# Sixteen output gates of a hybrid decoder layer, moved from the heads' stage into a Strassen product by token

## The chip, the cores and the metric

One core of a Trainium2 chip runs the whole layer as one program. The metric is the device time of one launch in microseconds; the kernel before takes 2931.25 us (median of three runs, 2930.26 to 2932.18). Names of engines: PE is TensorE, DVE is VectorE, ACT is ScalarE, POOL is GpSimd, SP is SyncE, whose queue issues every DMA of this kernel.

## The reference

One layer on 512 tokens of width 2048, float32. After an adaptive RMS norm, h is multiplied by one wide matrix w_in whose columns feed all that follows:

- a sliding-window attention branch with 32 query heads, gated by silu and projected to y_a;
- a gated DeltaNet branch with 16 key heads and 32 value heads of 128 columns. A causal convolution and silu give q, k and v, a recurrence over chunks gives o for each value head, and then

```python
o = rms_norm(o, dn_norm_w) * silu(dz.reshape(B, T, DN_V_HEADS, DN_HEAD_V))
y_b = o.reshape(B, T, DN_VAL) @ w_o_dn
```

- a merge y = sigmoid(mg_a) * y_a + sigmoid(mg_b) * y_b, and x + gate * (y @ w_out).

The change concerns dz = h @ w_in[:, 12800:16896], 128 columns for each value head: the output gates.

## The kernel before, in words

**Products.** h lies transposed in SBUF (channels on partitions, tokens along the row) as two parts, hh (rounded to a shorter format) and hl (the rest). A weight is split the same way: ACT rounds a half tile of 128 x 1024 into whi (split, L52) and DVE subtracts into wlo (L53). Each product of such operands takes three matmuls (mm3, L237): high by high, high by low, low by high. A **channel tile** (channel_tile, L244) computes 128 output channels for all 512 tokens: 16 steps over the input channels, 48 matmuls into one PSUM bank. `plan` (L158) lists the weight tiles in the order of use; raw tiles of 1 MB are loaded two ahead (load_job, L195), their halves are split with three buffers (split_half, L204).

**Order of work.** Everything that hangs beside the large products is written as a generator, and `pump` (L81), called after every second step of a channel tile (eight times per tile), advances it: `live` generators count their waits in calls of pump, `slow` ones (the triangular solve) have a budget per call, and `side` ones (beside, L78) a rate per call. The program's scheduler then orders each engine's instructions by this order and by when it expects their inputs.

**The heads' stage** (deltanet, L590; heads, L788). For each of 16 key heads g there are five channel tiles: the queries q, two value heads v, and two gates z. `queries` (L818) runs the convolution, transposes, masks (POOL, L714 and L715), the product pqk (L869), the assembly of the inverse, and then `scan` (L898), the recurrence over four chunks, in which PE, DVE and ACT take turns. `zgate` (L797) turns a z tile into silu times the norm's weight, still with channels on partitions. At the end of scan the two heads' results in osb (tokens on partitions) are scaled by the norm (L968), turned on PE (transpose4, L271, tiles pto), multiplied by the gate on DVE (L975) and stored to o_d (L979). The solve of the second half of the heads runs as a slow generator in groups 0 to 7 and is drained at g = 8 (L643).

**Behind it** branch_b (L982) loads o_d head by head (L996), splits it, runs merge tiles ma5 to ma8 and multiplies by w_o_dn; attention (L1063) runs ma9 to ma15 at its end (L1101), while the last heads finish; finish (L1271) ends with the output product (output, L1326). That product is already a Strassen step: 512 x 2048 x 2048 as seven products of quadrants (256 tokens, 1024 input channels, 1024 output columns, in two column halves of 512). Its **items** are twelve matmuls of 128 x 512 each, four items to a product (m1 to m7), with tokens as output partitions. Weight quadrants lie in three slots a, b, c and are summed in place on DVE (L1347).

Of the kernel before, what the change touches and what calls it, by code (L numbers as in the profile page):

```python
# [16 lines left out]
P = 128  # L17
# [16 lines left out]
STW = 320 + NST * P  # L34


class Layer:
# [120 lines left out]
    def plan(self):  # L158
        a, jobs = self.a, []
        wi = lambda name, t: jobs.append((name, a["w_ch"][t]))  # L160
        jobs += [(f"st{u}", a["w_st"][u]) for u in range(KT // 2)]
        for j in range(NFIRST):
            wi(f"mb{j}", 96 + j)
        for kind, j in self.mixed():
            wi(f"{kind}{j}", (16 if kind == "k" else 96) + j)
        ma = lambda r: [wi(f"ma{j}", 146 + j) for j in r]
        ma(range(0, 3))
        for g in range(KH):
            wi(f"q{g}", g)
            for e in (2 * g, 2 * g + 1):  # L170
                wi(f"v{e}", 32 + e)
            for e in (2 * g, 2 * g + 1):
                wi(f"z{e}", 64 + e)
        ma(range(3, 5))
        for half in range(2):
            ma(range(5 + 2 * half, 7 + 2 * half))
# [8 lines left out]
        ma(range(9, 16))  # L185
        jobs += [(f"os{j}", a["w_os"][j]) for j in range(KT)]
        self.jobs = jobs

    def prime(self):
        self.job_load = self.half_split = self.half_used = 0  # L190
        self.raws, self.halves, self.due = {}, {}, []
        for _ in range(2):
            self.load_job()

    def load_job(self):  # L195
        j = self.job_load
        if j < len(self.jobs):
# [6 lines left out]
    def split_half(self):  # L204
        n = self.half_split
        j = n // 2
        if j < len(self.jobs):
# [7 lines left out]
            if n % 2:  # L215
                del self.raws[j]
                self.due.append(self.load_job)

# [25 lines left out]
    def channel_tile(self, name, xh=None, xl=None):  # L244

        xh, xl = (self.hh, self.hl) if xh is None else (xh, xl)
        ps = self.pmm.tile([P, T], F32, tag="mm", name="mm")
# [29 lines left out]
    def build(self):  # L277
        tc, nc, a = self.tc, self.nc, self.a
        with ExitStack() as es:
# [26 lines left out]
            if self.stop == "deltanet":  # L306
                return
            self.gate_d = self.dram.tile([D], F32, name="gate_d")
# [9 lines left out]
    def consts(self):  # L318
# [20 lines left out]
        nc.vector.tensor_scalar(out=self.dnwh, in0=self.dnw, scalar1=0.5, scalar2=None, op0=ALU.mult)  # L339
        yield  # L340
# [249 lines left out]
    def deltanet(self):  # L590
# [8 lines left out]
        self.o_d = dram.tile([VH, P, T], F32, name="o_d")  # L599
        with ExitStack() as ps:  # L600
# [34 lines left out]
            with ExitStack() as sb:  # L635
# [12 lines left out]
                self.drain_live()  # L648
        self.dump("o", self.o_d)
# [138 lines left out]
    def heads(self, wk, g):  # L788
# [5 lines left out]
        for e in range(2):  # L794
# [12 lines left out]
    def values(self, wk, g, e, ps, st):  # L807
# [6 lines left out]
        vt = wk.tile([P, NTB, P], F32, tag="vt", name="vt", bufs=3)  # L814
# [3 lines left out]
    def queries(self, wk, g, ps, st):  # L818
# [22 lines left out]
        for e in range(2):  # L841
            h = 2 * g + e
            qe = wk.tile([P, NTB, P], F32, tag="qe", name="qe", bufs=2)
# [54 lines left out]
    def scan(self, wk, g, k, kT, TT, qd, M, epsq, st):  # L898
# [3 lines left out]
        osb = wk.tile([P, 2, NTB, P], F32, tag="osb", name="osb", bufs=1)  # L902
# [53 lines left out]
        while len(z) < 2:  # L956
# [9 lines left out]
        for e in range(2):  # L966
# [3 lines left out]
            )  # L970
        yield 2
# [8 lines left out]


    def branch_b(self):  # L982
        tc, nc, a = self.tc, self.nc, self.a
        with ExitStack() as es:
# [8 lines left out]
            for half in range(2):  # L993
# [4 lines left out]
                for j in range(2):  # L998
                    self.merge_gate("ma", 5 + 2 * half + j, self.ma_d)
# [63 lines left out]
    def attention(self):  # L1063
        tc, nc, a = self.tc, self.nc, self.a
        with ExitStack() as es:
# [35 lines left out]
            for j in range(9, KT):  # L1101
# [388 lines left out]
def layout(i):  # L1490
# [18 lines left out]
    o["w_ch"] = f(np.concatenate([ch(w_in[:, 4608:16896]), ch(w_in[:, 19008:]), ch(w_in[:, :2304]), ch(w_in[:, 2560:4608]), ch(w_in[:, 16960:19008])]))  # L1509
    o["w_os"] = f(ch(i["w_o_swa"][0]))  # L1510
# [57 lines left out]
```

## Time and profile before

| what | value |
|---|---|
| median of 3 runs | 2931.25 us |
| span of the profiled execution (the page gives it no other time) | 2929.7 us |
| PE, DVE, ACT, POOL busy | 98%, 61%, 37%, 8% of the span |
| heads' stage, one steady period | 67.31 us |
| output stage, first and second column half | 90.5 and 78.7 us |
| loads and stores | 451.11 MB, mean 154 GB/s |

How to read it: a row of the profile names a line of the kernel, an engine, an operation, the tile written and the tiles read; then come the count, the busy time, the mean of one in nanoseconds, the idle time of the engine just before, and what ended that idle time. A stretch row gives its length and then the busy time and the instruction count of each engine, the granted clock of PE (1.00 is full), the DMA engines' busy share and their rate. Consecutive matmuls overlap, so the busy time of one (0.39 us) is more than its share of the time.

### The profile page before, as it was taken

The numbers are of one execution on the slowest core, as the hardware profiler recorded it, in microseconds if no ns is written. First come the engines' busy times: TensorE is split into PE (matmuls) and PEld (weight loads), VectorE is DVE, ScalarE is ACT, GpSimd is POOL, SyncE is SP. The second block draws the span as 40 slices with busy tenths as digits, with TensorE's granted clock in tenths as the row PEclk, the third lists the DMA queues.
The fourth block names the chain that finished last, engine by engine and source line by source line (L and its number), as shares of the span: only waits on it lengthen the run. The fifth ranks groups of instructions, "written<-read, shape, count | busy, mean of one in ns | idle before, by whom it ended". The sixth has DMA issues, their size and how long they took to land.

```text
span 2929.7 us, 38073 instructions
## 1 busy us (share of the span) xinstructions
PE 2870.6 (98%) x14556; PEld 2351.2 (80%) x14556; DVE 1787.2 (61%) x2915; ACT 1085.1 (37%) x2113; POOL 243.0 (8%) x204
## 2 busy tenths in 40 slices
PE   8899999999999999999999999999999999999988
PEld 6677888888888888888888788888787877888867
DVE  6775998777776545544444553434655655553697
ACT  4355333333334333333333322212343443432343
POOL 0022211100000110000000000000100000000022
PEclk9999999999999999999999999999999999999999
DMA  9747555633334533333332675554322223375562
GB/s 387 281 147 219 163 169 159 203 109 111 125 113 134 160 116 124 115 122 109 123 109 100 235 263 182 186 172 141 105 89 94 85 89 103 119 262 172 173 194 97
DMA packets 175046, 451.11 MB, mean 154 GB/s; under 512 B 72433, under 2 KB 74993, under 8 KB 138897
## 3 DMA queue, kind: packets, MB, share of 16 engines
q1 hardware_dynamic: 174866, 448.70, 46.1%
q8 instruction: 114, 1.87, 0.3%
q14 instruction: 66, 0.54, 0.1%
HBM read 386.95 MB, written 59.45 MB: 152 GB/s over the span
## 4 chain that ended last, share of the span: by engine, by line
PE 84%; DVE 3%; DMA 2%; issue 1%; ACT 1%; POOL 1%; SPq 0%; POOLq 0%; DVEq 0%; ACTq 0%
PE mm L240 24%; PE mm L242 24%; PE mm L241 24%; DVE wlo L53 1%; PE S L1208 1%; PE pv L918 1%; PE po L937 1%; PE O L1259 1%; PE pP L274 1%; PE po L936 1%; PE pd L933 1%; PE pp L908 1%; PE m L241 1%; PE m L242 1%; PE m L240 1%
## 5 line engine op out<-in xcount | busy, mean ns | idle before, releaser
L240 PE MATMUL mm<-hh,whi 128*128 128x512 f32 x2784 | 1130.7, 406 | 2.3 <-ACT whi L52 1.6
L242 PE MATMUL mm<-hh,wlo 128*128 128x512 f32 x2784 | 1089.6, 391 | 1.3 <-DVE wlo L53 1.3
L241 PE MATMUL mm<-hl,whi 128*128 128x512 f32 x2784 | 1087.3, 391 | 0.0
L53 DVE TENSOR_TENSOR wlo<-raw,whi 128x1024 fp32r<-128x1024 f32 (+1 forms) x452 | 554.4, 1229 | 491.5 <-ACT whi L52 481.7
L52 ACT CAST whi<-raw 128x1024 fp32r<-128x1024 f32 (+1 forms) x452 | 470.7, 1044 | 972.9 <-PE mm L241 927.3
L242 PEld LDWEIGHTS mm<-hh,wlo 128*128 128x128 f32 x2784 | 522.6, 188 | 115.1 <-DVE wlo L53 2.2
L240 PEld LDWEIGHTS mm<-hh,whi 128*128 128x128 f32 x2784 | 523.7, 188 | 112.3 <-issue 8.4
L241 PEld LDWEIGHTS mm<-hl,whi 128*128 128x128 f32 x2784 | 524.2, 188 | 98.7 <-issue 0.4
L240 PE MATMUL mm<-oh,whi 128*128 128x512 f32 x512 | 200.6, 393 | 2.6 <-ACT oh L52 1.7
L242 PE MATMUL mm<-oh,wlo 128*128 128x512 f32 x512 | 199.4, 390 | 0.5 <-DVE wlo L53 0.5
L241 PE MATMUL mm<-ol,whi 128*128 128x512 f32 x512 | 199.5, 390 | 0.1
L865 POOL TENSOR_TENSOR qe<-qe,yq 128x512 f32<-128x512 f32 x32 | 51.4, 1624 | 902.7 <-DMA qe<-eg_rows 836.9
L714 POOL TENSOR_TENSOR E<-E,neg_g 128x512 f32<-128x512 f32 x64 | 78.4, 1224 | 476.2 <-DMA E<-g_rows 342.8
L240 PEld LDWEIGHTS mm<-oh,whi 128*128 128x128 f32 x512 | 96.0, 188 | 24.8 <-ACT oh L52 3.0
L241 PEld LDWEIGHTS mm<-ol,whi 128*128 128x128 f32 x512 | 96.1, 188 | 22.2 <-DVE ol L53 1.3
L764 DVE TENSOR_TENSOR A<-A,atmp 128x62 f32<-128x62 f32 (+30 forms) x124 | 112.9, 911 | 1.5
L242 PEld LDWEIGHTS mm<-oh,wlo 128*128 128x128 f32 x512 | 96.1, 188 | 20.9 <-DVE wlo L53 1.3
L757 DVE TENSOR_TENSOR atmp<-A 128x62 f32<-128x62 f32 (+30 forms) x124 | 109.3, 882 | 1.5
L911 DVE SCALAR_TENSOR_TENSOR r<-pp,neg_eg,vt 128x128 f32<-128x128 f32 x96 | 29.2, 346 | 78.8 <-PE pp L908 77.6
L1232 ACT ACTIVATE sm<-sm,mx,rs 128x256 f32<-128x256 f32 (+1 forms) x128 | 71.7, 561 | 3.3 <-DVE mx L1227 3.3
L580 DVE SCALAR_TENSOR_TENSOR yv<-mm,convh,yv 128x511 f32<-128x511 f32 (+2 forms) x96 | 71.5, 745 | 1.6
L241 PE MATMUL m<-wlo,hh 128*128 128x512 f32 x128 | 51.8, 404 | 10.1 <-DVE wlo L53 10.1
(331 smaller groups left out, 3145.6 us busy)
## 6 DMA issues: line engine op xcount, KB each, us to landing
raw<-in_w_ch SPq DMA_DIRECT2D x158, 1024.0 KB
wa<-in_w_ada_ss SPq DMA_DIRECT2D x32, 1024.0 KB
raw<-in_w_od SPq DMA_DIRECT2D x32, 1024.0 KB
E<-g_rows SPq DMA_DIRECT2D x64, 256.0 KB
gw<-in_w_ada_gate SPq DMA_DIRECT2D x16, 1024.0 KB
raw<-in_w_os SPq DMA_DIRECT2D x16, 1024.0 KB
qe<-eg_rows SPq DMA_DIRECT2D x32, 256.0 KB
o_d<-zh SPq DMA_DIRECT2D x32, 256.0 KB
```

Source lines behind the costliest of these rows:

```text
L52: self.nc.scalar.copy(out=hi, in_=src)
L53: self.nc.vector.tensor_tensor(out=lo, in0=src, in1=hi.bitcast(F32), op=ALU.subtract)
L240: nc.tensor.matmul(ps, lhsT=wh, rhs=xh, start=first, stop=False)
L241: nc.tensor.matmul(ps, lhsT=wh, rhs=xl, start=False, stop=False)
L242: self.last_mm = nc.tensor.matmul(ps, lhsT=wl, rhs=xh, start=False, stop=last).ins
L274: self.nc.tensor.transpose(dst[:, c * P : (c + 1) * P], src_cols(c), self.ident)
L580: nc.vector.scalar_tensor_tensor(out=y[:, s:], in0=ps[:, : T - s], scalar=w[:, j : j + 1], in1=y[:, s:], op0=ALU.mult, op1=ALU.add)
L714: nc.gpsimd.tensor_tensor(out=E, in0=E, in1=ng, op=ALU.add)
L757: eng.tensor_tensor(out=t, in0=A[:, m : m + 1, m + 1 :].to_broadcast([P, m, n]), in1=A[:, :m, m : m + 1].to_broadcast([P, m, n]), op=ALU.mult,
L764: eng.tensor_tensor(out=A[:, :m, m + 1 :], in0=A[:, :m, m + 1 :], in1=t, op=ALU.add)
L865: nc.gpsimd.tensor_tensor(out=qf, in0=qf, in1=q, op=ALU.mult)
L1232: nc.scalar.activation(t, t, AF.Exp, scale=r[:, h : h + 1], bias=mx[:, h : h + 1], accum_out=den[:, h : h + 1])
```

## The change

The gates of value heads 12 to 27 (key heads 6 to 13, `ZG`) leave the heads' stage. Their 2048 columns become one product of 512 x 2048 x 2048 in a new stage, zstage, between deltanet and branch_b.

- In groups of ZG heads runs three channel tiles, not five. The scan no longer turns and gates: it stores the scaled osb by token to ot_d, two DMAs per group. Buffers: vt 3 to 4, qe 2 to 4, osb 1 to 2.
- token_sums, a side generator from group 8 on at 0.14 steps per call of pump, makes the four combinations of quadrants of h (s1 to s4) on POOL, DVE and ACT, in four chunks, and stores them as high and low parts (32 stores of 256 KB); the quadrant of h that s1 will replace is saved (two stores of 1 MB).
- zstage loads the weight slots and the sums, runs ma5 (moved here from branch_b) and then 56 items. The sums of weights are issued four items ahead: a+b on DVE, b+c, a+c and b+a on POOL. A finished quadrant is gated by token: tanh on ACT, a multiply-add on DVE, a product with the loaded o on POOL; two items later four transposes on PE, a scaled copy on ACT and the store to o_d. s1 takes the place of a quadrant of hh and hl, which is loaded back in the second half.
- The list of weight loads pauses at zstage and resumes at its end (rejoin). Merge tiles: ma5 to zstage, ma6 to ma9 in branch_b, ma10 to ma15 in attention.

```diff
+Z0 = 12
+ZG = range(Z0 // 2, Z0 // 2 + 8)
...
-            for e in (2 * g, 2 * g + 1):
+            for e in (2 * g, 2 * g + 1) if g not in ZG else ():
                 wi(f"z{e}", 64 + e)
-        ma(range(3, 5))
+        ma(range(3, 6))
+        self.apart = len(jobs)
+        jobs += [(f"za{i}", a["w_z"][0, i]) for i in range(2)]
...
                     if g == 8:
                         self.drain_slow(s1)
+                        self.beside(self.token_sums(sol1), 0.14, "sums")
...
+        if g in ZG:
+            yield 1
+            for e in range(2):
+                k, i = divmod(2 * g + e - Z0, 4)
+                nc.sync.dma_start(
+                    out=self.ot_d[k].rearrange("c p n -> p c n")[:, :, i * P : (i + 1) * P], in_=osb[:, e]
+                )
+            return
...
+            order = [
+                ("m1", "a11", "a", []), ("m7", "s3", "b", ["ab", "bc"]), ("m5", "s1", "a", []), ("m2", "a12", "b", []),
+                ("m6", "s2", "a", ["ac"]), ("m4", "a22", "b", ["ba"]), ("m3", "s4", "c", []),
+            ]
...
+            def weight_sums(i):
+                if i < len(items):
+                    _, m, p = items[i]
+                    for x, y in order[m][3]:
+                        eng = nc.vector if (x, y) == ("a", "b") else nc.gpsimd
+                        eng.tensor_tensor(out=piece(x, p), in0=piece(x, p), in1=piece(y, p), op=ALU.add)
...
+            def turned(k, t, src, scale):
+                pt = pf.tile([P, T], F32, tag="tp", name="ptz", bufs=2)
+                self.transpose4(pt, lambda h: src[:, h * P : (h + 1) * P])
+                oz = wk.tile([P, T], F32, tag="w", name="oz")
+                nc.scalar.activation(oz, pt, AF.Copy, scale=scale)
...
+            def gated(i, n, c, t, src, neg):
+                k = 2 * c + n
+                o = wk.tile([P, T], F32, tag="o", name="ot")
+                nc.sync.dma_start(out=o, in_=self.ot_d[k, t])
+                th = wk.tile([P, T], F32, tag="w", name="zth")
+                nc.scalar.activation(th, src, AF.Tanh, scale=-0.5 if neg else 0.5)
+                nc.vector.scalar_tensor_tensor(out=src, in0=th, scalar=1.0, in1=src, op0=ALU.add, op1=ALU.mult)
+                nc.gpsimd.tensor_tensor(out=src, in0=src, in1=o, op=ALU.mult)
+                late.append((i + 2, k, t, src, self.dnwn if neg else self.dnwh))
...
+                    elif name == "m6":
+                        u1, u5 = keep["m1", t], keep["m5", t]
+                        u = wk.tile([P, T], F32, tag="m", name="u2", bufs=3)
+                        TT(out=u, in0=b, in1=u1, op=ALU.add)
+                        TT(out=u1, in0=ps["m7", t], in1=u, op=ALU.add)
+                        x = wk.tile([P, T], F32, tag="m", name="c22", bufs=3)
+                        TT(out=x, in0=u1, in1=u5, op=ALU.add)
+                        TT(out=u5, in0=u, in1=u5, op=ALU.add)
+                        gated(i, n, 1, 2 + t, x, False)
...
+            load("b", 1, 0, 0)
+            load("c", 1, 1, 0)
+            for n in ("s3", "s2", "s4"):
+                sums(n)
+            pm = self.channel_tile("ma5", ps=pf.tile([P, T], F32, tag="tp", name="ma", bufs=2))
+            th = wk.tile([P, T], F32, tag="w", name="mth")
+            nc.scalar.activation(th, pm, AF.Tanh, scale=0.5)
+            nc.sync.dma_start(out=self.ma_d[5], in_=th)
+            sums("s1")
+            todo = []
+            for i in range(2):
+                slots["a", i] = self.raws.pop(self.apart + i)
...
+                    if kk == 0:
+                        prep(i + 2)
+                        weight_sums(i + 4)
+                        for f in todo:
+                            evict(i, *f)
+                        todo = []
+                        while late and late[0][0] <= i:
+                            turned(*late.pop(0)[1:])
+                if p == 3:
+                    todo.append((n, name))
```

More of the change, by code (lines that the diff above doesn't have):

```diff
@@ L339, in consts @@
         nc.vector.tensor_scalar(out=self.dnwh, in0=self.dnw, scalar1=0.5, scalar2=None, op0=ALU.mult)
+        self.dnwn = const.tile([P, 1], F32, name="dnwn")
+        nc.vector.tensor_scalar(out=self.dnwn, in0=self.dnw, scalar1=-0.5, scalar2=None, op0=ALU.mult)
         yield
@@ L648, in deltanet @@
                 self.drain_live()
+                self.drain("sums")
         self.dump("o", self.o_d)
@@ L901, in scan @@
         v = [st["v0"], st["v1"]]
[L902 removed]
+        osb = wk.tile([P, 2, NTB, P], F32, tag="osb", name="osb", bufs=2)
         osq = wk.tile([P, 2, NTB], F32, tag="osq", name="osq")
@@ L955, in scan @@
         z = st["z"]
-        while len(z) < 2:
+        while g not in ZG and len(z) < 2:
             yield 1
```

179 lines of the change are left out of this document (168 added, 11 removed).

## The prediction

> **What bounds the kernel now.** I read the page's busy shares and its chain first, then stretches of the span by engine, and last the waits and the order of instructions in the stages that the change touches.
>
> ```profile
> span 2929.7 us, 38073 instructions
> ...
> PE 2870.6 (98%) x14556; PEld 2351.2 (80%) x14556; DVE 1787.2 (61%) x2915; ACT 1085.1 (37%) x2113; POOL 243.0 (8%) x204
> ...
> PE 84%; DVE 3%; DMA 2%; issue 1%; ACT 1%; POOL 1%; SPq 0%; POOLq 0%; DVEq 0%; ACTq 0%
> ```
>
> TensorE (PE) is busy for 98% of the span and is 84% of the chain that ended last. The stretches (length, then busy time of each engine with its instructions) show it by stage:
>
> ```profile
> core 0: us, PE busy (x) PEld busy (x) DVE busy (x) ACT busy (x) POOL busy (x), PEclk, DMA share, GB/s
> ...
> 1369.08:1436.39 67.31, 67.31 (x359) 56.03 (x358) 33.52 (x63) 25.12 (x57) 6.45 (x6) 1.00 0.37 119
> 1834.00:2047.00 213.00, 213.00 (x937) 174.95 (x936) 85.73 (x101) 48.56 (x52) 1.00 (x2) 1.00 0.50 167
> 2568.00:2580.00 12.00, 11.25 (x50) 8.98 (x49) 11.22 (x17) 11.13 (x18) 0.00 (x0) 1.00 1.00 355
> 2752.00:2842.50 90.50, 80.37 (x335) 64.03 (x335) 85.85 (x131) 42.10 (x63) 7.73 (x5) 0.94 0.62 201
> 2842.50:2921.20 78.70, 77.12 (x339) 63.16 (x338) 68.56 (x66) 29.36 (x30) 26.23 (x9) 1.00 0.33 106
> ```
>
> The first row is one period of the heads' stage (one key head, two value heads): PE never stops. The second, nearly all large products, gives their price: 213.00 us / 937 = **0.2273 us** each. The last two are the two column halves of the output product, which is already a Strassen step. It is the only place with idle PE time to speak of, and the nearest row for what is added.
>
> **What goes and what comes on PE.** Sixteen gate tiles of 16 x 3 products leave the heads: 768 x 0.2273 = 174.6 us. The new stage has 2 halves x 7 products x 48 = 672, 152.7 us. Gain **21.8 us**. The 64 transposes of these heads move along and cost the same (eight took 1.26 us), and so does the merge tile ma5.
>
> ```profile
> 1626.86 1.26 PE pto L274 x8
> ```
>
> So everything hangs on whether PE stays fed.
>
> **The heads' stage.** A period in groups 6 to 13 falls from 67.31 by 2 x 10.9 and the transposes' 1.3 to about 44.2 us. The scan is emitted by calls of pump, now 24 a group and not 40; from a query tile's end to the last scan step I count some 51, so two groups' scans overlap more. The steps' distance in calls stays, so each has as much PE time over it as before, and the larger buffer counts (vt, qe, osb) fit the overlap. A busier VectorE (DVE) is the risk: 33.52 us less the gates' work (per group four subtractions of weights at 1.24 and four operations of a gate at 0.68, as in these two groups of instructions) is 25.9 in 44.2, 59%, and token_sums adds about 22 us of DVE and 31 of GpSimd (POOL) over groups 8 to 14 (32 operations at 0.68, 24 at the 1.29 below).
>
> ```profile
> L53 DVE TENSOR_TENSOR wlo<-raw,whi 128x1024 fp32r<-128x1024 f32 x436 | 538.1, 1237 | 484.9 <-ACT whi L52 475.2 <-PE pqk L869 5.7 <-PE pgate L1483 3.7
> ...
> L804 DVE SCALAR_TENSOR_TENSOR zh<-zth,zh 128x512 f32<-128x512 f32 x32 | 21.9, 684 | 0.0
> ```
>
> The nearest rows are the early groups, in which the triangular solve keeps DVE fuller still (one product per group starts at these times):
>
> ```profile
> 627.04 0.89 PE pqk L869 x8
> 694.35 0.89 PE pqk L869 x8
> 762.70 0.89 PE pqk L869 x8
> 830.00 0.89 PE pqk L869 x8
> ...
> 1369.08 0.89 PE pqk L869 x8
> ```
>
> Periods of 67.31, 68.35 and 67.30 against the quiet 67.31: at most 1 us lost per group. I take 0.4 for eight groups, **3 us** (0 to 8). The solve itself still ends in time: its last store is issued in group 6, before the forced drain at group 8.
>
> ```profile
> 972.23 1.18 SPq L784 DMA_DIRECT2D ts_d<-A  x2
> ```
>
> SyncE's (SP's) queue gets two stores of osb per group and 34 of sums; what stands behind them are loads a period ahead, and I cost them at nothing. If that cover fails, E and qe are late, and with them the ceiling of 8.
>
> **The new stage: DVE and POOL.** In the old output stage DVE makes all sums of weights; here POOL makes three of four, and multiplies by the heads' result. How these two get on shows in single instructions:
>
> ```profile
> 2850.39 10.36 POOL L1400 TENSOR_TENSOR m<-m,x 128x512 f32<-128x512 f32 x1 [4.52 <-DMA x<-in_x]
> ...
> 2850.44 1.22 DVE L1347 TENSOR_TENSOR raw<-raw,rawb 128x1024 f32<-128x1024 f32 x1
> 2851.58 1.22 DVE L53 TENSOR_TENSOR wlo<-rawb,whi 128x1024 fp32r<-128x1024 f32 x1
> 2852.72 1.22 DVE L1347 TENSOR_TENSOR rawb<-rawb,rawc 128x1024 f32<-128x1024 f32 x1
> ...
> 2859.65 2.18 DVE L53 TENSOR_TENSOR wlo<-rawb,whi 128x1024 fp32r<-128x1024 f32 x1
> ...
> 960.86 3.69 POOL L865 TENSOR_TENSOR qe<-qe,yq 128x512 f32<-128x512 f32 x2 [67.00 <-DMA qe<-eg_rows]
> 961.07 4.55 DVE L777 TENSOR_TENSOR A<-A,bet 128x1024 f32<-128x1024 f32 x2
> ...
> 2904.28 1.29 POOL L1400 TENSOR_TENSOR c<-c,x 128x512 f32<-128x512 f32 x1 [8.54 <-DVE c L1397]
> ...
> 2902.86 0.69 DVE L1425 TENSOR_TENSOR m<-u,m 128x512 f32<-128x512 f32 x1
> 2903.46 0.69 DVE L1397 SCALAR_TENSOR_TENSOR c<-c,gt 128x512 f32<-128x512 f32 x1
> ```
>
> A POOL product of 512 columns takes 1.29 us alone, 10.36 while DVE adds without a gap; a DVE subtraction of 1.22 takes 2.18 when POOL gets in; two of each at 960.86 take turns. They exclude each other. The Trainium skill (SBUF — State Buffer, Who interferes with whom) says so too: a VectorE instruction with two SBUF inputs and a GpSimd instruction that reads SBUF block one another for a whole instruction. By that rule the sums given to POOL are no free second pair of hands, which speaks against this change; the rows agree.
>
> So I add up, per half, what the two need together. Starts in a row give DVE 1.14 us per 1024 columns and 0.60 per 512. POOL's 1024 columns are not in the trace: between 1.29 and twice that, 2.58; I take 2.4, near the upper end, as DVE's own 0.60 and 1.14 nearly double. POOL: 12 x 2.4 + 8 x 1.29 = 39.1. DVE with two SBUF inputs: 28 subtractions and 4 sums x 1.14 + 12 x 0.60 = 43.7. Together **82.8 us**; PE needs 336 x 0.2273 + 32 x 0.16 = 81.5. By the Trainium skill (GPSIMD Engine Reference, 3. Performance versus the Vector engine: 4497 ns for 2048 columns) a sum would be an estimated 2.25, and the total 81.0 instead.
>
> How full can such a pair run? The old second half did (28 + 16) x 1.14 + 12 x 0.60 + 8 x 1.29 = 67.7 in 77.9 us, 87%, and PE waited 1.4:
>
> ```profile
> PE m L241 <- DVE wlo L53: 10.1, 5, 5.9
> ...
> PE m L241 <- DVE wlo L53: 1.4, 1, 1.4
> ```
>
> (The first row is the first half, where DVE makes the operands as well.) At 87% the new half takes 95 us, 13.5 over PE; at 100% 82.8, 1.3 over. The bursts sit around m7 and around m4 and m6, with the weights two items ahead as slack; I take **9 us a half, 18 in all** (3 to 27). ScalarE's queue holds casts behind the tanh of each gate, and PE's transposes stand behind the whole chain DVE, tanh (0.59), DVE, POOL; both are in the 9, since only the chain's lateness against two and a half items (6.8 us) counts. An item, twelve products, is the 2.72 us between two casts:
>
> ```profile
> 2886.50 1.05 ACT L52 CAST whi<-raw 128x1024 fp32r<-128x1024 f32 x1 [1.66 <-PE m L242]
> 2889.22 1.06 ACT L52 CAST whi<-raw 128x1024 fp32r<-128x1024 f32 x1 [1.67 <-PE m L242]
> ...
> L263 ACT ACTIVATE mth<-mm x32: 573/590/632, 156.3 to 2577.4; 128x512 f32<-128x512 f32 x32
> ```
>
> **Its start and end.** The new tiles lie in memory that the last group releases:
>
> ```profile
> L975 DVE TENSOR_TENSOR zh<-pto,zh x32: 677/681/691, 619.7 to 1629.1; 128x512 f32<-128x512 f32 x32
> ```
>
> That is some 4 us after ma5's start. Then b, c, s3, s2, s4 and s1 queue, 12.6 MB: at 355 GB/s (share 1.00 in the row above) 35 us, so s1 is there 39 to 41 us after ma5's start. PE wants it after ma5 and eight items, 10.9 + 21.8 = 32.7, plus a few us of waits: **5 us** (0 to 8). At the end the last gate's chain (two sums 0.60, two tanh, two products, POOL 1.29, transposes, copy) is about 6 us; if the next stage's first bank waits for it, PE stands: **4 us** (0 to 6.5). In attention one merge tile fewer (48 calls, not 56) covers the last group; its last products ended at 2566.2 and the last merge's tanh began at 2577.4 (row above), so of 11 us of cover about none is left: **0.5** (0 to 2).
>
> ```profile
> 2564.31 1.90 PE O L1259 x32
> ```
>
> **Sum.** -21.8 + 3 + 18 + 5 + 4 + 0.5 = **+8.7 us**. On the profiled span, 2929.7, this is 2938.4. The page gives that execution no time beside its span; the median of the runs, 2931.25, is 1.55 above it, so **2940**.
>
> **Rivals.**
> *The cover holds (faster).* Each half waits as little as the old second half, 1.4, because the sums are asked for four items ahead and POOL runs early; s1 is in time and the end is covered: -21.8 + 2.8 + 1 + 1 = -17, **2914**. For it: DVE has half of its time free in the heads, and twelve sums fewer per half here. Against: 82.8 us of mutual exclusion in 81.5.
> *POOL starves and PE stands at the transposes (slower).* Place: m6, where four additions per tile, tanh, gating and POOL's product must be done before PE's turn. Without interference the second tile's source is ready 2.3 (cast and subtraction) + 10 x 0.60 + 1.29 = 9.6 us after the product ends, and PE is there at 6.8 + 0.6 = 7.4; with two sums of 2.4 in between it is 14.4, a wait of 7. With 3 at m3 and 7 at m7 (four sums by each engine and four subtractions, 18.8 us against 10.9 of PE) a half loses 17; two halves and 6 + 6 + 4 for start, end and heads give -21.8 + 50 = +28, **2959**. It decides from where POOL's product starts over 4 us after its inputs.
> *The saving is not collected.* If the scans, not PE, pace the thinner groups, each returns 2.7 us of its 23: -21.8 is gone in the heads alone, and with the stage's waits **2962**.
>
> **Chances.** Forecast (2930 to 2950) 0.47; cover holds 0.25; starved 0.22; not collected 0.06. A difference under 0.2% (5.9 us) can't be told from none. Between 2925.4 and 2937.1 I put 0.13 of the forecast and 0.03 of the first rival: same 0.16, faster 0.22, slower 0.34 + 0.22 + 0.06 = 0.62. Range 2918 to 2962: it leaves out the better half of the first rival (0.13) and the tail of the last two (0.07).
>
> **What would show it.** Periods of 44 to 45 us between the pqk products of groups 7 to 13, not 47, show the gain collected. POOL sums of 2.4 us, several of 4 or more, and DVE subtractions of 2.3 to 3.6 show exclusion. Waits of PE for wlo and for the transposes' sources of 14 to 22 us in all in the new stage, and its length of 185 us without ma5, show the bill. I am wrong if POOL's sums run beside DVE's subtractions at full speed, if the order written by the scheduler keeps all gates off PE's path, or if the loads at the start land in under 33 us.

## The result, and the profile after

The changed kernel takes **2984.5 us** (median of 4 runs, 2979.5 to 2986.9); the kernel before took 2930.8 beside it (4 runs). The ratio is 1.0181, with a 95% interval of 1.0167 to 1.0196. The prediction, 2940 with a range of 2918 to 2962, is outside: right in its sign, 44 us too low.

The page of the changed kernel, in the lines that were shown of before:

```profile
span 2980.9 us, 38256 instructions
...
PE 2870.3 (96%) x14460; PEld 2344.2 (79%) x14460; DVE 1928.4 (65%) x2992; ACT 1124.6 (38%) x2161; POOL 393.9 (13%) x268
...
PE 75%; DVE 6%; DMA 5%; POOL 2%; issue 2%; ACT 1%; SPq 0%; POOLq 0%; DVEq 0%; ACTq 0%
```

PE issues 96 matmuls fewer, as it should, and its busy time is nearly the same; it is less of the chain (75%, not 84%). To see where the time went, I cut both spans at the same work: the product pqk of group 5 (the last with all its gates), the last transposes of the heads (pto), the last of the new stage (ptz). The start of before's first mark; the last heads' transposes of before stand in the prediction, at 1626.86:

```profile
897.77 1.05 PE L869 MATMUL pqk<-yq,kT 128*128 128x128 f32 x8
```

And the changed kernel's three marks (start, length, engine, line; in brackets PE's idle time before and what ended it):

```profile
895.04 1.05 PE L889 MATMUL pqk<-yq,kT 128*128 128x128 f32 x8
...
1484.50 1.26 PE L286 MATMUL pto<-ident,osb 128*128 128x128 f32 x8 [1.30 <-DVE osb L988]
...
1687.82 2.34 PE L286 MATMUL ptz<-ident,m 128*128 128x128 f32 x8 [4.71 <-POOL m L1145]
```

- **Heads.** From pqk to pto before took 1626.86 - 897.77 = 729.1 us, after 589.5: 139.6 less. Gone from PE were 174.6 us of products and the 64 transposes, 10.1, together 184.7. So **45 us were lost in the heads**, where the prediction had 3.
- **New stage.** From the end of pto (1485.76) to the end of ptz (1690.16) are 204.4 us. Its work is ma5 (10.9), 152.7 of products and 10.1 of transposes, 173.7. **31 us were lost**; the prediction had 18 + 5 + 4 = 27. PE is idle for 24 of them; the other 7 go with the granted clock, 0.98 and 0.92 in the two parts below.
- **The rest.** Behind it lie 2980.9 - 1690.2 = 1290.7 us; before, without ma5, 2929.7 - 1628.1 - 10.9 = 1290.7. Nothing was lost there (the prediction had 0.5). The groups ahead of the first mark were 2.7 us shorter.

The waits of PE over the whole run (total, number, longest) name the places:

```profile
PE pd L953 <- DVE vs L945: 28.0, 12, 3.7
...
PE m L253 <- DVE wlo L55: 13.4, 8, 5.3
PE ptz L286 <- POOL c L1145: 10.7, 7, 3.4
PE ptz L286 <- POOL m L1145: 8.6, 3, 4.7
```

The first is a wait that the kernel before doesn't have: a step of the scan, in which PE wants vs. The second was there, mostly in the output stage; only 2.9 us of it lie in the new stage. The last two are the new transposes, which wait for the gate's product on POOL.

Stretches of the changed kernel: groups 6 and 7, two periods of later groups, and the new stage in two parts:

```profile
963.46:1020.34 56.88, 49.88 (x249) 40.47 (x248) 44.09 (x59) 22.78 (x52) 29.55 (x20) 0.91 0.54 173
1020.34:1073.57 53.23, 44.96 (x246) 37.02 (x246) 42.16 (x71) 22.17 (x55) 19.18 (x14) 0.97 0.56 190
...
1073.57:1120.39 46.82, 44.69 (x254) 37.23 (x253) 26.50 (x56) 18.58 (x48) 7.84 (x6) 1.00 0.41 126
1120.39:1168.77 48.38, 46.26 (x254) 38.51 (x253) 26.47 (x56) 18.67 (x48) 7.73 (x6) 0.96 0.38 121
...
1496.50:1596.00 99.50, 89.21 (x391) 71.59 (x389) 81.85 (x56) 43.53 (x50) 52.69 (x21) 0.98 0.60 217
1596.00:1691.00 95.00, 81.25 (x347) 64.75 (x347) 70.20 (x52) 40.34 (x48) 47.04 (x20) 0.92 0.40 123
```

So the heads have two losses of different kinds. In groups 6 and 7 a period is 57 and 53 us, with DVE busy for 44 and 42 of them. In the six periods from 1073.57 to 1358.97 it is 47.6 on the mean (285.4 / 6) where 44.2 was forecast, though DVE has nearly half of its time free. Against the 44.4 us that such a period takes without a wait (run 13), the first two lose 21 us and the six 19; the remaining 4 lie in the period behind them, 71.7 us where before's were 67.3. In the last two rows PE is idle for 10.3 and 13.75 us, and its granted clock is under 1.00.

**Three theories, with rivals.** A: the token sums come as one burst in groups 6 to 8. C: in the later groups some queue holds up the scan, not the scan's work. D and E: in the new stage PE waits for the gate's chain, and that is late because DVE and POOL exclude each other. The rival of A and C is B: without gates the scans themselves are too long for the period.

### The profile page after: what moved, and what is told of

It reads as the page before. It is cut to its first block, busy times and chain, and to the rows that moved or that the text cites. A ratio compares the mean times of both kernels' runs of the same rounds, so it can differ in the third digit from the quotient of the medians.

```text
span 2980.9 us, 38256 instructions
## 1 busy us (share of the span) xinstructions
PE 2870.3 (96%) x14460; PEld 2344.2 (79%) x14460; DVE 1928.4 (65%) x2992; ACT 1124.6 (38%) x2161; POOL 393.9 (13%) x268
## 4 chain that ended last, share of the span: by engine, by line
PE 75%; DVE 6%; DMA 5%; POOL 2%; issue 2%; ACT 1%; SPq 0%; POOLq 0%; DVEq 0%; ACTq 0%
PE mm L252 21%; PE mm L254 21%; PE mm L253 20%; DVE wlo L55 2%; DMA E<-g_rows 2%; PE m L254 1%; PE m L253 1%; PE m L252 1%; PE S L1454 1%; PE po L957 1%; PE O L1505 1%; PE pP L286 1%; PE pd L953 1%; PE pv L938 1%; POOL E L734 1%
## 5 line engine op out<-in xcount | busy, mean ns | idle before, releaser
L252 PE MATMUL mm<-hh,whi 128*128 128x512 f32 x2512 | 1024.1, 408 | 2.3 <-ACT whi L54 1.6
L254 PE MATMUL mm<-hh,wlo 128*128 128x512 f32 x2512 | 985.8, 392 | 1.1 <-DVE wlo L55 1.1
L253 PE MATMUL mm<-hl,whi 128*128 128x512 f32 x2512 | 984.5, 392 | 0.0
L55 DVE TENSOR_TENSOR wlo<-raw,whi 128x1024 fp32r<-128x1024 f32 (+1 forms) x444 | 584.3, 1317 | 439.4 <-ACT whi L54 434.7
L252 PEld LDWEIGHTS mm<-hh,whi 128*128 128x128 f32 x2512 | 475.2, 189 | 103.5 <-issue 8.4
L254 PEld LDWEIGHTS mm<-hh,wlo 128*128 128x128 f32 x2512 | 473.6, 189 | 104.8 <-DVE wlo L55 1.9
L253 PEld LDWEIGHTS mm<-hl,whi 128*128 128x128 f32 x2512 | 475.5, 189 | 89.4 <-issue 0.4
L253 PE MATMUL m<-wlo,hh 128*128 128x512 f32 x256 | 102.6, 401 | 9.0 <-DVE wlo L55 9.0
L254 PE MATMUL m<-whi,hl 128*128 128x512 f32 x256 | 101.8, 398 | 0.9 <-DMA hl<-s_d 0.9
L252 PE MATMUL m<-whi,hh 128*128 128x512 f32 x256 | 101.7, 398 | 0.0
```

The lines of the kernel that those rows point to most:

```text
L55: self.nc.vector.tensor_tensor(out=lo, in0=src, in1=hi.bitcast(F32), op=ALU.subtract)
L252: nc.tensor.matmul(ps, lhsT=wh, rhs=xh, start=first, stop=False)
L253: nc.tensor.matmul(ps, lhsT=wh, rhs=xl, start=False, stop=False)
L254: self.last_mm = nc.tensor.matmul(ps, lhsT=wl, rhs=xh, start=False, stop=last).ins
```

## The experiments

Each run was timed beside the kernel before on the same chip; ratios are to that, and differences from the changed kernel are differences of the ratios (1.0181 less the run's) times 2931 us. Where no edit touches a stage, that stage kept its length within 5 us.

### The burst in groups 6 to 8 (runs 1 and 2)

All operations of the token sums write the tile tsum. Two of their six groups on POOL in the changed kernel (count; shortest, median and longest in ns; first and last start):

```profile
L1033 POOL TENSOR_TENSOR tsum<-hh x4: 1299/1737/1740, 976.1 to 1026.7; 128x512 f32<-128x512 f32 x4
...
L1050 POOL TENSOR_TENSOR tsum<-tsum,hh x4: 1288/1480/1727, 993.6 to 1053.9; 128x512 f32<-128x512 f32 x4
```

All four chunks were done by 1056 us, in group 7, although the generator is advanced at 0.14 steps per call from group 8's emission on. Nothing ties a step to the product beside it; the scheduler puts it where it expects its inputs, and those were there as soon as the solve had stored its half (at 970).

**Run 1** leaves the sums' arithmetic out and keeps their stores, with other data in them (the product is then another one):

```diff
-            for i, v in enumerate((H, L)):
-                PT(out=x[i], in0=v[:, k, lo], in1=v[:, k, hi], op=ALU.add)
-                PT(out=x[2 + i], in0=v[:, k, hi], in1=v[:, u, hi], op=ALU.subtract)
...
+            for n in ("s3", "s1", "s2", "s4"):
+                for j, v in enumerate((H, L)):
+                    nc.sync.dma_start(out=self.ts_sum[n][j, :, k, :], in_=v[:, k, hi])
```

> The token sums' arithmetic is left out of the heads (their 34 stores stay and carry other data, so the product comes out otherwise). Theory A (their 32 VectorE, 24 GpSimd and 16 ScalarE operations come as one burst behind the solve, 963 to 1063 us of the changed kernel, and PE waits for vs there): the periods of groups 5 to 8 fall from some 54 us to the 47 of the later groups, the waits of PE for vs lose the 16 us of that stretch, and the time falls by 14 to 22 us. Rival B (the groups without gates are paced by their scans, whatever lies beside them): the waits move on, and the time falls by 0 to 5 us.

Measured: 2964.5 us, ratio 1.0116 (1.0094 to 1.0138), 19 us less than the changed kernel. The periods from group 6 on are 43.2, 46.8, 46.8 and 48.4 us. Theory A: the burst costs 19 us; the later periods stay.

**Run 2** keeps all the sums, and ties each step behind the product that PE has reached when it is due (the same tie falls on attention's one side generator; the stages behind the heads kept their length):

```diff
-                if next(q[0][0], True):
+                with self.behind():
+                    done = next(q[0][0], True)
+                if done:
                     q.pop(0)
```

> The same token sums, but each step is tied behind the product that PE has reached when the step is due, so that they spread over groups 8 to 14 as the prediction had them. Theory A (the burst costs, not the work): the time falls by 10 to 18 us, with periods of 47 to 49 us from group 7 on. Rival B (their work costs the same wherever it lies, as VectorE and GpSimd exclude one another): 0 to 5 us either way.

Measured: 2958.3 us, ratio 1.0089 (1.0072 to 1.0105), 27 us less (10 to 18 were expected); its profiled span is 20.1 less. That is at least as much as leaving the work out (the intervals of the two runs overlap). In its trace one of the POOL groups of the sums, and two periods:

```profile
L1052 POOL TENSOR_TENSOR tsum<-tsum,hh x4: 1285/1286/1297, 1076.4 to 1362.7; 128x512 f32<-128x512 f32 x4
```

```profile
963.98:1007.22 43.24, 43.24 (x242) 35.83 (x241) 24.97 (x41) 18.43 (x43) 9.28 (x8) 1.00 0.42 134
1007.22:1052.68 45.46, 44.69 (x254) 37.29 (x253) 29.79 (x60) 19.10 (x50) 7.50 (x7) 1.00 0.56 175
```

The sums are now spread over some 400 us, and the first period behind the solve has no idle PE at all. For the sums alone (tile tsum), in the changed kernel and in run 2: the stretch, its length, the busy time of DVE, ACT and POOL, then the clock and the DMA engines:

```profile
970.00:1070.00 100.00, 31.13 (x32) 9.92 (x16) 36.08 (x24) 0.93 0.56 185
```

```profile
980.00:1410.00 430.00, 22.80 (x32) 9.83 (x16) 33.77 (x24) 0.98 0.45 143
```

The same operations take 8 us less on DVE and 2 less on POOL. The place was what cost; the work itself costs little (run 14, below, has what is left).

### The later groups (runs 3, 5, 9 and 13)

One step of a scan in the changed kernel, group by group the same. In the order of time: SP issues the load of E, POOL masks it, PE has done pv, ACT takes the two exponentials of E and only then copies vn, DVE scales vs, and PE goes on:

```profile
1179.44 0.80 SPq L727 DMA_DIRECT2D E<-g_rows  x2
...
1184.54 1.98 POOL L734 TENSOR_TENSOR E<-E,neg_g 128x512 f32<-128x512 f32 x1 [37.04 <-DMA E<-g_rows]
...
1185.63 0.60 PE L938 MATMUL pv<-vt,tt 128*128 128x128 f32 x4
...
1187.26 0.63 ACT L879 ACTIVATE E<-E 128x512 f32<-128x512 f32 x1 [2.75 <-POOL E L735]
1188.99 0.63 ACT L879 ACTIVATE E<-E 128x512 f32<-128x512 f32 x1 [1.09 <-POOL E L735]
1189.52 0.35 ACT L940 COPY vn<-pv 128x256 f32<-128x256 f32 x1
...
1189.91 0.29 DVE L945 TENSOR_SCALAR vs<-vn,kd 128x128 f32<-128x128 f32 x1 [2.85 <-ACT vn L940]
...
1191.10 0.70 PE L953 MATMUL pd<-vs,k 128*128 128x256 f32 x2 [2.13 <-DVE vs L945]
```

pv ends at 1186.23; vn could start then, and starts at 1189.52, behind two instructions of the next group that wait for their mask. The wait named in PE's row is DVE's vs, but the holder is two engines back: ACT's queue. E's load itself waits for the last product that reads its buffer and lands 5 us later, so I first took the late load for the cause.

**Run 3** gives E a third pair of buffers (the gates' tiles z, idle in these groups):

```diff
-        M = [self.decay_load(wk, 2 * g + e) for e in range(2)]
+        M = [self.decay_load(wk, 2 * g + e, *(("z", 2) if g in (8, 11) else ())) for e in range(2)]
```

**Run 5** also emits load and mask sooner:

```diff
+        M = [self.decay_load(wk, 2 * g + e, *(("z", 2) if g in (8, 11) else ())) for e in range(2)]
         yield from self.conv(wk, ps, g, q)
-        M = [self.decay_load(wk, 2 * g + e) for e in range(2)]
+        for e in range(2):
+            self.decay_mask(M[e], 2 * g + e)
```

**Run 9** emits the load behind that of the k of the group before, and the mask behind that group's Y:

```diff
         nc.sync.dma_start(out=k.rearrange("p c d -> p (c d)"), in_=self.k_d[g])
+        if g + 1 in range(8, 14):
+            self.pre[g + 1] = [
+                self.decay_load(wk, 2 * g + 2 + e, *(("z", 2) if g in (7, 10) else ())) for e in range(2)
+            ]
```

> The decay tiles E of groups 8 and 11 lie in the gates' tiles z, which are idle there, so that E of groups 8 to 13 can be loaded a group earlier. Theory C (in the steady thin groups the chain is: po frees E, E is loaded in 5.0 us, masked on GpSimd, exponentiated on ScalarE ahead of vn, and PE waits 2.1 us for vs, after which the granted clock drops in every second group): the periods of groups 9 to 13 fall from 46.8 and 48.4 to 44.2 to 45.2, and the time by 8 to 16 us. Rival B (the scans pace): the same periods within 0.5 us, 0 to 3 us in all.

> As the third run (E of groups 8 and 11 in the idle z tiles), and E is loaded and masked as soon as its query's product is done, ahead of the convolution and of the transposes. In the third run the clock stayed at 1.00 but PE still waited 1.6 us per group for vs, behind ScalarE, which waited 2.9 us for a mask of GpSimd. Theory C (the late E, not the scan, holds ScalarE): periods of groups 8 to 13 of 44.2 to 45.2 us, the waits of PE for vs in 1110 to 1300 us near 0, and the time 12 to 20 us under the changed kernel's (the third run gave 9). Rival B (the scan's own steps pace): 46.3 as in the third run, 8 to 10 us in all.

> E of groups 8 to 13 is loaded and masked a whole group ahead (three groups' E in memory by the idle z tiles). In the fifth run the E loads were still issued late, 16 us behind pqk, since they stand in SyncE's queue behind the two stores of osb, which wait 2.5 us for VectorE; the exponentials of E then waited 2.9 us on ScalarE, with vn behind them, and PE waited 1.63 us per group for vs. Theory C2 (that queue is the whole cause): ScalarE's waits for E in 1110 to 1300 us go, periods of 44.2 to 45 us in groups 8 to 13, and a time 16 to 22 us under the changed kernel's. Rival F (ScalarE's own work between pv and vn, the sums of squares and a cast, keeps vn late): PE still waits 1 us or more per group, periods of 45.5 to 46.3, 9 to 13 us.

Measured: 2977.3, 2975.3 and 2977.6 us; ratios 1.0153 (1.0136 to 1.0169), 1.0152 (1.0138 to 1.0166) and 1.0155 (1.0141 to 1.0169). Each is some 8 us less than the changed kernel, with most periods of groups 8 to 11 at 46.3: half of what theory C asked, and no more in runs 5 and 9 than in run 3. The rows of run 5 show why:

```profile
1184.70 0.94 SPq L995 DMA_DIRECT2D ot_d<-osb  x2
1185.70 1.39 SPq L727 DMA_DIRECT2D E<-g_rows  x2
...
1196.75 0.63 ACT L879 ACTIVATE E<-E 128x512 f32<-128x512 f32 x1 [2.94 <-POOL E L735]
...
1201.87 0.70 PE L953 MATMUL pd<-vs,k 128*128 128x256 f32 x2 [1.63 <-DVE vs L945]
```

The load did not come earlier but later. In the changed kernel it stands ahead of the two stores of osb (1179.44 against 1183.94), 3.7 us behind the start of the last vn of the scan before; in run 5 the scheduler put it behind them, 9.2 us after that vn, and so it did in runs 3 and 9 (stores at 1181.77 and 1186.01, loads at 1182.76 and 1187.01). And it still put each exponential right where it expected the mask, so ACT waited 2.94 us and vn behind it. So none of the three runs got the earlier load that they were made for. Neither the expectation of run 9 (SP's queue is the whole cause) nor C as first put (the late load) was put to the test by them.

**Run 13** leaves E as in the changed kernel and holds the exponentials at their place in the program, behind the query's sums of squares:

```diff
+        with self.behind():
-        for e in range(2):
-            nc.scalar.activation(M[e], M[e], AF.Exp)
+            for e in range(2):
+                nc.scalar.activation(M[e], M[e], AF.Exp)
```

> The exponentials of E keep their place in the program, behind the products that PE has reached by then (behind the query's sums of squares), in place of being hoisted to where their mask is expected. Theory C3 (ScalarE's queue: an exponential waits 2 to 2.9 us for GpSimd's mask and vn stands behind it, so PE waits for vs): PE's waits for vs in 1110 to 1300 us under 1 us, periods of groups 9 to 13 of 44.2 to 45 us, the clock at 1.00 in each, and a time 15 to 25 us under the changed kernel's. Rival F (the scan's chain itself is longer than PE's work beside it): periods of 46.3 or more, 0 to 10 us.

Measured: **2960.4 us**, ratio 1.0098 (1.0084 to 1.0112), 24 us less. ACT's rows, and the stretch over four groups (length, then busy time of PE, PEld, DVE, ACT, POOL, the clock, DMA):

```profile
1193.73 0.37 ACT L941 COPY vn<-pv 128x256 f32<-128x256 f32 x1
...
1200.68 1.15 ACT L880 ACTIVATE E<-E 128x512 f32<-128x512 f32 x2
...
1203.60 0.37 ACT L941 COPY vn<-pv 128x256 f32<-128x256 f32 x1 [1.77 <-PE pv L939]
```

```profile
1110.00:1300.00 190.00, 190.00 (x1075) 159.73 (x1074) 113.57 (x233) 80.44 (x204) 31.03 (x24) 1.00 0.42 131
```

The exponentials run without a wait between two vn, PE is not idle for a moment, and the periods are 44.42 to 44.45. Nothing else was changed, so the two exponentials in ACT's queue held the scan, and rival B (the scans are too long) is out. By the marks of the traces 19 of the 24 us lie in the heads; the new stage, which the edit doesn't touch, was 4 shorter.

### The new stage (runs 4, 6, 7 and 10)

**Run 4** stores the products as they are; tanh, gating, POOL's product and the turning are left out, so the heads' results aren't gated:

```diff
-                o = wk.tile([P, T], F32, tag="o", name="ot")
...
-                nc.gpsimd.tensor_tensor(out=src, in0=src, in1=o, op=ALU.mult)
-                late.append((i + 2, k, t, src, self.dnwn if neg else self.dnwh))
+                h = Z0 + 4 * k
+                nc.sync.dma_start(
+                    out=self.o_d[h : h + 4].rearrange("h p t -> p h t")[:, :, t * P : (t + 1) * P],
+                    in_=src.rearrange("p (h t) -> p h t", h=4),
+                )
```

> The new stage stores its products as they are: tanh, gating, GpSimd's product and the turning by 64 transposes are left out. Their PE work is 64 x 0.16 = 10 us. Theory D (the stage's waits are those of the transposes for the gate's chain, 19.3 us in the changed kernel, and the clock granted after them): the time falls by 29 to 36 us. Rival E (the weights' sums and subtractions of VectorE and GpSimd alone fill the stage, by mutual exclusion): PE then waits for wlo in place of the transposes, and the time falls by 10 to 18 us.

Measured: 2958.1 us, ratio 1.0085 (1.0069 to 1.0101), 28 us less, just under the range of theory D; 10 of these are the transposes' work. So 18 us hang on the gate's chain, but POOL's products, a part of theory E, are gone with it: this run doesn't part the two.

**Run 6** writes the turned result over its source, so that tanh needn't wait for a store to free its tile:

```diff
-                oz = wk.tile([P, T], F32, tag="w", name="oz")
+                oz = src
```

> In the new stage the turned result is written over its source, so that the tanh of a gate no longer shares its two tiles with results that wait to be stored. Theory D1 (the tanh waits for the store of the result, 2 to 2.7 us behind each pair of gates, and PE's transposes with it): the waits of PE for the transposes' sources fall from 19.3 to 6 to 12 us and the time by 8 to 15 us. Rival D2 (the chain is late by itself: additions on VectorE, tanh, product on GpSimd among the weights' sums): 0 to 4 us.

Measured: 2985.9 us, ratio 1.0184 (1.0170 to 1.0197): no difference, and PE's waits for the transposes' sources stay (19.2 us, 19.3 in the changed kernel). D1 falls: the tile was not what the chain waited for, though the chain of waits passes through that store.

**Run 7** gives POOL's sums to DVE (the first edit); **run 10** its products too (both), so that POOL does nothing in the stage:

```diff
-                        eng = nc.vector if (x, y) == ("a", "b") else nc.gpsimd
+                        eng = nc.vector
...
-                nc.gpsimd.tensor_tensor(out=src, in0=src, in1=o, op=ALU.mult)
+                nc.vector.tensor_tensor(out=src, in0=src, in1=o, op=ALU.mult)
```

> VectorE makes all sums of weights of the new stage, as in the old output stage; GpSimd keeps only the products with the heads' result. Theory E (exclusion: a sum of 2.4 to 6.8 us on GpSimd holds up both engines, one on VectorE takes 1.14): the stage gets 6 to 14 us shorter. Rival D2 (the gates' chain counts, and VectorE at 24 more sums of 1.14 us is later with it): 0 to 8 us longer.

> GpSimd does nothing in the new stage: VectorE makes all sums of weights and the gates' products (per half 44 x 1.14 + 20 x 0.60 = 62 us of its time in 81.5 of PE). Theory E (exclusion of the two engines is the stage's loss, by the sums and by the products): the seventh run's 8.5 us become 14 to 20 us, and the waits for the transposes' sources fall from 12.5 to under 5 us. Rival D2 (the chain of a gate is late by its order behind the casts and subtractions): 6 to 11 us, about as the seventh run.

Measured: 2977.2 us, ratio 1.0150 (1.0137 to 1.0164), and 2966.7, ratio 1.0123 (1.0105 to 1.0142): 9 and 17 us less. The changed kernel's sums on POOL by line, and a group of subtractions on DVE in the stage (count, busy, mean ns):

```profile
L1102 POOL TENSOR_TENSOR rawzb<-rawzb,rawzc x8: 2389/3314/3372, 1499.3 to 1604.2; 128x1024 f32<-128x1024 f32 x8
L1102 POOL TENSOR_TENSOR raw<-raw,rawzc x8: 2372/2394/3390, 1518.6 to 1624.1; 128x1024 f32<-128x1024 f32 x8
L1102 POOL TENSOR_TENSOR rawzb<-rawzb,raw x8: 3263/3378/3392, 1532.9 to 1637.5; 128x1024 f32<-128x1024 f32 x8
```

```profile
L55 DVE TENSOR_TENSOR wlo<-raw,whi 128x1024 fp32r<-128x1024 f32 x25 | 52.1, 2092 | 15.8 <-ACT whi L54 15.8
```

The same group in run 10, and what is left of PE's waits for the transposes there:

```profile
L55 DVE TENSOR_TENSOR wlo<-raw,whi 128x1024 fp32r<-128x1024 f32 x28 | 34.3, 1224 | 26.5 <-ACT whi L54 26.5
```

```profile
PE ptz L286 <- DVE m L1145: 5.7, 2, 4.3
```

The shortest sums on POOL take 2.4 us and the medians of two of the lines 3.3 and 3.4, while the subtractions on DVE take 2.09 on the mean. With POOL silent DVE does 24 sums and 16 products more, and each subtraction is back at 1.22. The stage's loss falls from 31 to 10 us (1488.7 to 1672.3 is 183.6, less 173.7). Theory E holds in this: two thirds of the loss come from sharing this work with POOL. How much of it is exclusion and how much POOL's own slower pace (2.4 us for a sum that DVE does in 1.22) was not taken apart. Of what is left, 4.3 us are the last gate at the end and 4 are hh and hl, whose loads land late.

### Together (runs 8, 11, 12, 14 and 15)

**Run 8** joins runs 2, 5 and 6 and turns one item later (`late.append((i + 3, ...))`); **run 11** joins runs 2, 9 and 10; **run 12** is run 11 with the results in place and the later turn.

> The paced token sums of the second run, the early E of the fifth, the results in place of the sixth, and the turning one item later. If the terms are separate (27 us of the burst, 12 to 20 of E, 8 to 15 in the new stage, against 53 us lost to the kernel before), the time is 2925 to 2945 us where the kernel before takes 2931; if PE's waits only move from one cause to the next, 2945 to 2960.

> Paced token sums, E a group ahead, and the new stage without GpSimd. If the three losses are separate (26, 16 to 22 and 8 to 20 us): 2920 to 2936 us where the kernel before takes 2931. If the heads' two causes are one (both are PE's waits for vs in the same groups): 2938 to 2948.

> The eleventh run, with the turned results in place of their source and the turning one item later. If the transposes' sources still come too late in the eleventh run, 3 to 8 us less than it; if VectorE's subtractions are then the wait (as in the eighth run, where the waits for wlo rose from 13.4 to 19.0 us as those for the transposes fell), the same within 3 us.

Measured: run 8 takes 2958.8 us, ratio 1.0090 (1.0076 to 1.0104), no better than run 2 alone. In the stage the waits for the transposes fell from 19.3 to 10.9 us and those for wlo rose from 2.9 to 10.2: a later turn only moves the wait while the two engines still share the work. Run 11 takes 2936.7, ratio 1.0016 (1.0008 to 1.0025), and run 12 2936.4, ratio 1.0014 (1.0005 to 1.0023): within 0.2% of the kernel before, and the same as each other.

**Run 14** joins runs 2, 3, 10 and 13 and loads s1 ahead of s2 and s4; **run 15** is that with the results in place and the later turn.

```diff
-            for n in ("s3", "s2", "s4"):
-                sums(n)
+            sums("s3")
...
-            sums("s1")
+            for n in ("s1", "s2", "s4"):
+                sums(n)
```

> Paced token sums, the exponentials in place, three groups of E, no GpSimd in the new stage, and s1 loaded ahead of s2 and s4. If C3 holds on top of the eleventh run (2936.7 us with the periods of groups 8 to 13 at 47 on the mean): 8 to 16 us less, 2920 to 2929 us, under the kernel before. If the eleventh run already has all that the exponentials cost: 2932 to 2937.

> The fourteenth run, with the turned results in place of their source and the turning one item later. The twelfth run showed no difference from the eleventh by this (2936.4 and 2936.7 us): the same as the fourteenth within 3 us.

Measured: run 14 **2923.7 us**, ratio **0.9968** (0.9956 to 0.9979), and run 15 2924.3, ratio 0.9972 (0.9960 to 0.9983). The change with these repairs is 9 us faster than the kernel before. Its page:

```profile
span 2922.1 us, 38168 instructions
...
PE 2852.4 (98%) x14460; PEld 2336.5 (80%) x14460; DVE 1911.8 (65%) x3032; ACT 1123.1 (38%) x2161; POOL 287.3 (10%) x228
```

PE is at 98% again. By the same marks (897.12, 1449.05, end of ptz 1630.61) its heads lose 7.5 us and its stage 6.6: -21.8 + 7.5 + 6.6 = -7.7, and its span is 7.6 shorter than before's. So the account closes. Of the 7.5 us, 4.9 are three stops of PE for vs, each with a token sum of some 2.25 us on POOL beside it and a subtraction of 1.64 to 2.00 on DVE ahead of vs; run 13, whose sums had all run by group 7, has no such stop in the later groups. So the spread sums still seem to cost these 5 us, though no run takes this apart. The single effects don't simply add: runs 2, 13 and 10 alone save 27, 24 and 17 us, together with the two smaller edits 62 (1.0181 - 0.9968).

## Why the prediction was wrong

- **Gain on PE, -21.8: right.** 96 matmuls fewer, each still 0.2273 us where PE is fed, and the span of run 14 adds up with it.
- **The heads' stage, 3 us (0 to 8): the step that failed.** It measured 45. Two sentences carried it. The first: "The steps' distance in calls stays, so each has as much PE time over it as before." A step did keep its distance, but not its neighbours. The trace of before shows it, in ACT's waits and in ACT's rows of one period:

```profile
ACT E L859 <- POOL E L715: 22.5, 8, 5.3
```

```profile
1184.35 0.37 ACT L920 COPY vn<-pv 128x256 f32<-128x256 f32 x1 [1.29 <-PE pv L918]
...
1215.64 0.37 ACT L920 COPY vn<-pv 128x256 f32<-128x256 f32 x1
...
1228.94 0.63 ACT L859 ACTIVATE E<-E 128x512 f32<-128x512 f32 x1 [4.96 <-POOL E L715]
```

  ACT stood 5.6 us per group at the same exponentials already, 22.5 us in the four groups of that view, and it cost nothing: the four vn of a scan lie 10.4 us apart, from 1184 to 1216, and then comes a hole of 36 us (to 1184.35 + 67.31) with no step of a scan in it, into which the exponentials fell. A period of 44.4 leaves 13 of these 36. The two gate tiles took the hole with them, and each wait of ACT now had a vn behind it. The prediction named the overlap of two scans, and asked of it only whether the buffers suffice. In run 13 this was 24 us, 19 of them in the heads' stretch of the trace.
- **The second sentence**, that the token sums add 22 us of DVE and 31 of POOL "over groups 8 to 14". They ran in groups 6 to 8. The prediction read the rate in the code and not who writes the queues; the early groups, which it took as the nearest rows, have a solve that is paced, and the sums were not. 19 to 27 us.
- **E and qe, "a period ahead", at nothing.** E was issued 5 us ahead of its mask, not a period. Whether an earlier E alone would have helped isn't shown, since no run got it earlier; with the late E in place and the order of ACT mended (run 13) nothing was lost. The prediction tied its ceiling of 8 to this cover and thought only of a late load, not of what stands behind its reader.
- **The stage, 18 + 5 + 4: near in sum, right in mechanism, less so in its parts.** 31 measured. A sum of 2.4 us on POOL was taken, and the shortest took 2.37 to 2.39; subtractions of 2.09 us on the mean against 1.22 show the exclusion. The rule of the Trainium skill that spoke against the change (SBUF — State Buffer, Who interferes with whom) agrees with these rows; giving POOL's work to DVE was worth 17 to 21 us of the 31 (run 10), of which POOL's own slower pace is a part that was not taken apart. The start was dearer in the forecast than in the trace (PE waited 0.9 us for hl, not 5), the end near (4.7, not 4), so the two halves lost about 25 and not 18. They lost it where the slower rival said, at the transposes (19.3 us of PE's waits, 2.9 for wlo), and the prediction had no term for the clock, some 7 us. In its check on the old second half 67.7 us stand against 77.9; its own row says 78.70, so 86% and not 87, which changes nothing.
- **The sign.** It didn't hang on luck: the stage alone, 31 against a gain of 21.8, makes the kernel slower. The size hung on the heads.
- **The rivals.** "The saving is not collected" had the place of a part of it (periods of 47.6, its mark for failure was 47) and a chance of 0.06, but the wrong mechanism: the scans didn't pace the groups. None of the rivals had two losses in the heads at once, and the range ended at the worst of them.

## What to carry to other kernels

When work leaves a stage, ask what ran in its shadow: list the waits of the engines that are not the bottleneck, and for each what stands next in that queue once the period is shorter. A wait that cost nothing in a long period becomes the path in a short one without any edit to it. And a rate or a place in the program is not a place in the queue: where a scheduler orders by readiness, a big piece of side work must be tied to the work beside it, or it comes at once.

## What the runs showed of the hardware

**A short stop costs the clock too.** Stretches of 3 us in the changed kernel, about 1 us behind the stops of 2.13, 2.12 and 2.13 us of three groups (the clock is the third number from the end):

```profile
1192.50:1195.50 3.00, 3.00 (x14) 2.44 (x14) 2.29 (x3) 0.92 (x6) 3.00 (x2) 1.00 0.00 0
1239.00:1242.00 3.00, 3.00 (x9) 2.40 (x8) 2.55 (x3) 1.33 (x6) 2.81 (x2) 0.50 0.00 0
1287.00:1290.00 3.00, 3.00 (x11) 2.51 (x10) 2.97 (x3) 1.75 (x6) 2.39 (x2) 0.52 0.00 0
```

Behind two of the three the clock is halved for about 3 us, in which PE issues 9 and 11 matmuls in place of 14; the period is then 48.4 and not 46.8, so a stop of 2.1 us costs 3.7. Of the five such stops in groups 8 to 12 three had this tail. In run 3 four stops of 1.63 to 1.81 us had none, and one of 1.86 had it (clock 0.50 from 1326.0 to 1329.2), while a stop of 1.86 in the changed kernel had none; with one tail in place of three, the clock is some 3 of the 8 us that run 3 gained. Between 1070 and 1400 us of the traces of the changed kernel and all its runs, none of 30 stops of 0.6 to 1.73 us had a tail, 9 of 21 of 1.80 to 1.95 us had one, and 21 of 34 of 2.06 to 2.17. What decides it for a single stop isn't shown. The Trainium skill (TensorE: Matmul & The Clock Gate, Part 1: The HAM clock gate) has the clock fall to half after an idle window of about 3.4 us. The half agrees (0.50); here stops of little more than half that length were enough, some of the time.

**The order of a queue is what counts.** That ACT takes its instructions strictly in turn is also in the Trainium skill (PSUM — Partial Sum Buffer, Engine vs sequencer instructions); run 13 shows its price, 24 us for two exponentials of 0.63 per group in the wrong place.
